# Weight low parts on VectorE in the front, later latent norms, earlier decays, a fifth bank and U tiles between the last queries

## The chip, the cores and the metric

One core of a Trainium2 chip runs the kernel. The metric is the device time of one execution in microseconds; a kernel's time is the median of several runs. Engines are named as in the profile: PE is TensorE's matrix engine, DVE is VectorE, ACT is ScalarE, POOL is GpSimd, SP issues most DMAs.

## The reference, cut to what matters

The input x has 512 rows (frames) of 1024 numbers, all float32. One layer is computed:

```python
h = rms_norm(x, g_mix);  proj = h @ w_in          # q_lat, kv_lat, k_rope, gq, gk, gv, g_lr, g_out, br
y_a = mla_attention(q_lat, kv_lat, k_rope, ...)    # norms of the latents, 8 heads, softmax
y_b = gla_mixer(gq, gk, gv, g_lr, g_out, ...)      # log_a = log_sigmoid(g_lr @ w_a2 + b_a2) / 16
x = x + (sigmoid(br_a) * (y_a @ w_branch_a) + sigmoid(br_b) * (y_b @ w_branch_b)) @ w_out
h = rms_norm(x, g_ffn)
s, idx = top_k(product_key_scores(h @ w_peer_q), 16)   # 8 heads x 2 halves, 128 keys each
y = sum over the best 16 experts of each head of gate * gelu(h . u[e]) * v[e]
out = rms_norm(x + y, g_final)
```

For 384 of the 512 rows the expert sum is computed densely over all 16384 experts (128 tiles of 128); the other 128 rows gather their experts' rows.

## The kernel before

**Products in three parts.** Every weight tile of 128x1024 float32 is loaded by SP into `raw` (3 buffers), split into a high part `whi` (ACT, `split_hi`, L236) and a low part `wlo` (`split_lo`, L242: raw minus high, on the engine in `lo_home[0]`, which is POOL until the dense U stage and DVE from there on). `mm3` multiplies with three matmuls for each of the 8 blocks: high with high, high weight with low activation, low weight with high activation. So the first two matmuls of a product `proj` need only `whi`; the third needs `wlo`. For the key tiles the order of operands is the other way and the second matmul needs the low part.

**Order.** The program is scheduled by hand: each engine runs its instructions in the order in which the code emits them. The weight tiles stand in one list (`want`): w1 tiles 0 to 5, the 8 key and value tiles `wkv`, w1 tiles 6 to 11, the query and key/value up-projections, gates, `wab`, `wo`, 16 `wpq` tiles, 128 `u` tiles. `weights(key)`, called at the start of a product, emits the low part of any tile whose high part is made already (`half`), then `run(1)`, one step of a list `later`; `further(key)`, called after the product, emits the high part of the tile after the next. So the low part of w1 tile k+1 is emitted at the start of product k, behind everything that the code emitted before it for the same engine.

**The front, in the order of the code.** Products 0 to 4 of w1 are the latents `ql`, each 24 matmuls into a bank of the PSUM group `pmm` (4 banks; `pk` and `pst` have 2 each). After product 2 the norm of x is made (`rstd`: a product with ones on PE, a DVE instruction, Ln and Exp on ACT with a table load before each, three DVE instructions), and three DVE multiplications evict products 0 to 2. After product 3 come its eviction and `rope_tables` (16 DVE instructions). Product 4 is evicted, then product 5 (`pm`) gives the gate's low-rank input and the rotary key: one small product, a copy `rcol`, six DVE instructions, then sums of squares of the latents (ACT squares, three DVE additions). Then the loop over 8 key tiles `c` (24 matmuls each; 4 banks `pv` of `pmm` and both of `pk` collect over all 8 tiles; POOL copies 32 rows of the rotary key in each). After tile 0 two `rstd` are started for the latents; their second halves and five latent norms (`latent_norm`: DVE, ACT, DVE) are put on `later`, one per following tile. After the loop `run()` empties `later`, ACT copies the four `pv` banks to `gv` (L511), four decay products with `wa2` follow (DVE `la`, ACT `z`), then Exp and Ln of `z`, a DVE instruction on `la`, and w1 products 6 and 7, the first of which takes the first bank of `pv`.

**The query stage.** For each of 16 `wpq` tiles: the product; for tiles 3 to 10 `normed(mt - 3)` (DVE multiplication, ACT high part, DVE low part of 128x384); ACT copies the product to `qq[mt]` (L909); `product_keys(mt - 1)`: PE multiplies by the keys, DVE makes top-16 values and indices for four row tiles (20 instructions). After the loop `some(P15)` runs 8 pieces (one U tile), `product_keys(15)`, then `some(3 * NC_D - P15)` two more U tiles; then `fx.close()` ends the front's SBUF pool, and `up_out` can evict the U products by a Gelu on ACT into `gx` (L975), which lies in a pool opened after that. `fill` then places U pieces by a cost count among the DVE work of `route` (the routing of the row tiles). What is left of the 128 U tiles goes in `trail` and among the `down` products at the end.

Of the kernel before, what the change touches and what calls it, by code (L numbers as in the profile page):

```python
# [10 lines left out]
F32 = mybir.dt.float32  # L11
# [5 lines left out]
AF = mybir.ActivationFunctionType  # L17
OP = mybir.AluOpType
# [20 lines left out]
PSH = ()  # L39
P15 = 8  # L40
G1, GO = 0.125, 0.5
LEAD = 3000.0
# [151 lines left out]
def body(ctx, tc, a, out):  # L194
# [32 lines left out]
    half = []  # L227
    lo_home = [pool]

# [61 lines left out]
    for mt in range(8):  # L291
        want(("wo", mt), a["wo"][mt].rearrange("p c m -> p (c m)"), 1024, v8)
    for mt in range(16):
        want(("wpq", mt), a["wpq"][mt].rearrange("p c m -> p (c m)"), 1024, v8)
    for e in range(128):
        want(("u", e), a["u"][e].rearrange("p c m -> p (c m)"), 1024, v8)
# [150 lines left out]
    for i in range(5):  # L447
        first.append(proj(("w1", i)))
        if i == 2:
            run()  # L450
            rstd(ssx, D, rX)
        if i >= 2:
            while first:
                dve.tensor_tensor(ql[i + 1 - len(first)], first.pop(0), rX, op=OP.mult)
        if i == 3:
            rope_tables()
# [17 lines left out]


    pv = [pmm() for _ in range(NT)]
    pk = [pmm("pk") for _ in range(2)]
    gv = fr.tile([128, NT, 512], F32, name="t6")
    kT = fr.tile([128, MH, T], F32, name="big2")
    for c in range(NC_D):  # L480
# [3 lines left out]
        for tt in range(NT):  # L484
# [4 lines left out]
            for n, (x, y) in enumerate(((0, 0), (0, 1), (1, 0))):  # L489
                pe.matmul(o, hs[x], w[y][:, 512:], start=f and tt % 2 == 0 and n == 0, stop=l and n == 2,  # L490
                          skip_group_check=True)
        if c == 0:
            rq = fr.tile([128, T], F32, name="rB", bufs=2)
# [13 lines left out]
            for i in range(5):  # L507
                later.append(lambda i=i: latent_norm(i))
    run()
    for tt in range(NT):  # L510
# [3 lines left out]
    further(("wkv", NC_D - 1))  # L514
    la = sb.tile([128, NT, 256], F32, name="la")
    z = sb.tile([128, NT, 256], F32, name="kd")
    for tt in range(NT):
        p = pmm("pst")
        pe.matmul(p[:, :256], lrT[0:GRANK + 1, tt * 128:(tt + 1) * 128], wa2, start=True, stop=True)
        dve.tensor_scalar(la[:, tt], p[:, :256], 0.0, 1.0 / TAU, op0=OP.min, op1=OP.mult)  # L520
        act.activation(z[:, tt], p[:, :256], AF.Abs)
    act.activation(z, z, AF.Exp, scale=-1.0)
# [315 lines left out]
    def normed(c):  # L838
        q = tmp()
        dve.scalar_tensor_tensor(q[:, GT:], x2[:, c, GT:], cc(C_GFFN + c), r2[:, GT:], op0=OP.mult, op1=OP.mult)  # L840
        split(h2d[c][0], h2d[c][1], q[:, GT:], dve)

# [56 lines left out]
    aside = [columns_of] + [lambda i=i: rows_of(i) for i in range(2)] + [lambda i=i: plain_rows_of(i) for i in range(2)]  # L899
    for mt in range(16):  # L900
        p = proj(("wpq", mt), h2x)
        if 3 <= mt < 3 + NC_D:
            normed(mt - 3)
        if mt > 2 and aside:
            aside.pop(0)()
        if mt == 0:
            rstd(ss, D, r2, defer=True)
        qq[mt] = tmp()
        act.activation(qq[mt], p, AF.Copy)  # L909
        if mt:  # L910
            product_keys(mt - 1)
    run()
    assert not aside
    ups = iter(range(128))
# [29 lines left out]
    def some(n):  # L944
        for _ in range(n):
            if left[0]:
# [3 lines left out]
                if c == NC_D - 1:  # L950
                    left[0] -= 1

    some(P15)
    product_keys(15)
    some(3 * NC_D - P15)
    lo_home[0] = dve
    ax = ExitStack()
# [9 lines left out]
    def up_out(keep=0):  # L967

        while len(pend) > keep:
            e, p = pend.pop(0)  # L970
            if e < NB[0]:
                g = pa.tile([128, ND], F32, name="gx", bufs=GX)
            else:
                g = ga[e] = dn.tile([128, ND], F32, name="gf", bufs=NF)
            act.activation(g, p[:, GT:], AF.Gelu)  # L975
            if e < NB[0]:
                act.dma_start(gad[e], g)


# [457 lines left out]
```

## Time and profile before

| | us |
|---|---|
| median of 3 runs (1653.6 to 1656.72) | 1655.02 |
| the profiled execution, its time | 1650.91 |
| its span from first to last instruction | 1649.1 |
| PE busy | 1611.3 |
| DVE busy | 1251.9 |
| ACT busy | 727.9 |
| POOL busy | 340.1 |

PE and DVE instructions are issued through a helper that counts their cost, so that nearly all of them have its line, L161; they are told apart by their tiles. The mean granted clock of TensorE was 0.995 of full speed. A matmul's row has its start and a modelled length; matmuls overlap, so the distance from start to start tells what one costs. A row with [x <-ENGINE tile] says that the engine was idle for x us before it, and who ended that.

### The profile page before, as it was taken

The page shows a single profiled execution, that of the slowest core. Times are in us where ns is not written, and L with a number is a line of the kernel's source. Part 1 is how long each engine was busy: PE and PEld are TensorE (multiplying, and loading weights), DVE is VectorE, ACT ScalarE, POOL GpSimd, SP SyncE. Part 2 cuts the span into 40 slices and gives each one's busy share as a digit, 9 for nine tenths or more (in the row PEclk, how much of TensorE's full clock was granted, in tenths as well). Part 3 has the DMA queues.
Part 4 walks back from the last instruction along what each step waited for, and adds up shares of the span by engine and source line. Part 5 has one row for each costly group of instructions (what it writes and reads, how often), then busy time and mean ns, then how long its engine had stood idle before and what let it go on. Part 6 is the DMA issues. An engine that isn't in the chain of part 4 may idle for free.

```text
span 1649.1 us, 23157 instructions
## 1 busy us (share of the span) xinstructions
PE 1611.3 (98%) x8505; PEld 1400.6 (85%) x8505; DVE 1251.9 (76%) x2528; ACT 727.9 (44%) x1251; POOL 340.1 (21%) x237
## 2 busy tenths in 40 slices
PE   7999999999989999999999999999999999999998
PEld 5777656888878899999999998888888888888876
DVE  6724575353789989988988747788888788888695
ACT  5442544334332645555555444344444444444343
POOL 4532143445324000000010001111111111112110
PEclk9999999999999999999999999999999999999999
DMA  5222112443332578878889998999999999999994
GB/s 178 64 77 77 52 58 90 168 146 98 132 103 90 188 277 282 285 277 309 278 302 336 331 369 312 332 370 342 396 340 384 347 380 351 397 329 360 346 343 150
DMA packets 156178, 414.11 MB, mean 251 GB/s; under 512 B 11975, under 2 KB 89928, under 8 KB 138016
## 3 DMA queue, kind: packets, MB, share of 16 engines
q1 hardware_dynamic: 121504, 234.02, 41.3%
q0 software_dynamic: 18576, 134.57, 21.7%
q10 hardware_dynamic: 15984, 44.05, 7.0%
q8 instruction: 66, 1.08, 0.3%
q14 instruction: 48, 0.39, 0.1%
HBM read 361.21 MB, written 51.38 MB: 250 GB/s over the span
## 4 chain that ended last, share of the span: by engine, by line
PE 83%; DVE 9%; DMA 2%; issue 2%; ACT 2%; POOL 0%; ACTq 0%; SPq 0%; DVEq 0%; POOLq 0%
PE pmm L161 59%; PE pst L161 13%; PE pk L161 11%; DVE kd L161 3%; DVE la L161 2%; DVE tmp L161 2%; DMA ga<-gad 1%; DMA gad<-gx 1%; DVE rB L161 0%; DVE r L161 0%; DVE act_lo L161 0%; ACT whi L236 0%; POOL wlo L242 0%; DVE rows L161 0%; DMA raw<-in_w 0%
## 5 line engine op out<-in xcount | busy, mean ns | idle before, releaser
L161 PE MATMUL pmm<-act_hi,whi 128*128 128x384 f32 (+1 forms) x992 | 355.5, 358 | 12.9 <-ACT act_hi L328 8.1
L161 PE MATMUL pmm<-act_hi,wlo 128*128 128x384 f32 (+1 forms) x992 | 347.6, 350 | 4.3 <-DVE wlo L161 4.3
L161 PE MATMUL pmm<-act_lo,whi 128*128 128x384 f32 (+1 forms) x992 | 347.3, 350 | 0.5 <-DVE act_lo L161 0.5
L996 POOL DMA_INDIRECT rows<-in_uv,gidx x128 | 132.9, 1038 | 935.9 <-DVE gout L161 884.7
L236 ACT ACTIVATE whi<-raw 128x1024 fp32r<-128x1024 f32 (+1 forms) x202 | 209.9, 1040 | 108.8 <-PE pmm L161 48.0
L242 POOL TENSOR_TENSOR wlo<-raw,whi 128x1024 fp32r<-128x1024 f32 (+1 forms) x77 | 182.4, 2371 | 292.5 <-ACT whi L236 255.8
L161 DVE TENSOR_TENSOR wlo<-raw,whi 128x1024 fp32r<-128x1024 f32 x125 | 152.7, 1222 | 87.3 <-ACT whi L236 85.7
L161 PEld LDWEIGHTS pmm<-act_hi,whi 128*128 128x128 f32 x992 | 188.4, 190 | 28.5 <-ACT act_hi L328 8.1
L161 PEld LDWEIGHTS pmm<-act_hi,wlo 128*128 128x128 f32 x992 | 188.1, 190 | 14.5 <-DVE wlo L161 4.9
L161 PE MATMUL pmm<-vlo,chi 128*128 128x512 f32 x512 | 199.9, 390 | 0.4 <-DVE vlo L161 0.2
L161 PE MATMUL pmm<-vhi,chi 128*128 128x512 f32 x512 | 199.4, 389 | 0.0
L161 PE MATMUL pmm<-vhi,clo 128*128 128x512 f32 x512 | 199.2, 389 | 0.0
L161 PEld LDWEIGHTS pmm<-act_lo,whi 128*128 128x128 f32 x992 | 188.4, 190 | 9.3 <-DVE act_lo L161 1.0
L161 DVE SCALAR_TENSOR_TENSOR gout<-rows,gact,gout 128x1024 f32<-128x1024 f32 x128 | 164.2, 1283 | 0.0
L161 DVE TENSOR_TENSOR vlo<-vraw,vhi 128x1024 fp32r<-128x1024 f32 x128 | 156.3, 1221 | 0.0
L161 DVE SCALAR_TENSOR_TENSOR rows<-rows,hrep 128x1024 f32<-128x1024 f32 x128 | 156.2, 1220 | 0.0
L1252 ACT ACTIVATE vhi<-vraw 128x1024 fp32r<-128x1024 f32 x128 | 134.0, 1049 | 26.3 <-DMA vraw<-in_v 25.8
L161 PE MATMUL pmm<-t,whi 128*128 128x512 f32 x448 | 141.8, 397 | 0.0
L161 PEld LDWEIGHTS pmm<-vlo,chi 128*128 128x128 f32 x512 | 96.1, 188 | 22.8 <-DVE vlo L161 2.9
L1008 ACT ACTIVATE gact<-gact 128x1 f32<-128x1 f32 x128 | 26.0, 203 | 197.8 <-DVE rows L161 197.7
L161 PEld LDWEIGHTS pmm<-vhi,clo 128*128 128x128 f32 x512 | 96.1, 188 | 18.7
L161 PEld LDWEIGHTS pmm<-vhi,chi 128*128 128x128 f32 x512 | 96.1, 188 | 18.6
(269 smaller groups left out, 2811.1 us busy)
## 6 DMA issues: line engine op xcount, KB each, us to landing
raw<-in_u SPq DMA_DIRECT2D x128, 512.0 KB
vraw<-in_v SPq DMA_DIRECT2D x128, 512.0 KB
gt<-gd SPq DMA_DIRECT2D x32, 768.0 KB
gd<-gs ACTq DMA_DIRECT2D x11, 2048.0 KB
gad<-gx ACTq DMA_DIRECT2D x96, 192.0 KB
ga<-gad SPq DMA_DIRECT2D x96, 192.0 KB
raw<-in_w SPq DMA_DIRECT2D x28, 512.0 KB
raw<-in_wpq SPq DMA_DIRECT2D x16, 512.0 KB
```

The costliest lines, as they stand in the source:

```text
L161: return f(*args, **kw)
L236: act.activation(hi[:, :n], raw[:, :n], AF.Copy)
L242: (lo_eng or lo_home[0]).tensor_tensor(lo[:, :n], raw[:, :n], hi[:, :n], op=OP.subtract)
L996: pool.indirect_dma_start(out=rows[n], out_offset=None, in_=a["uv"], in_offset=bass.IndirectOffsetOnAxis(ap=gidx[:, n:n + 1], axis=0))
L1008: act.activation(g, g, AF.Gelu)
L1252: act.activation(hi, vraw[n], AF.Copy)
```

## The change

1. `lo_home` starts with DVE, not POOL: all low parts up to the last `wo` tile are made by DVE. For the query stage it is set to POOL, as it was, and to DVE after it.
2. The fifth product of w1 goes to a bank of `pk`, not to the fifth place of `pmm`.
3. The two `rstd` of the latents and their five norms are queued after key tile 2, not after tile 0.
4. The four decay products, with their DVE and ACT instruction each, stand after key tiles 3 to 6 and no longer behind the loop and the `gv` copies; `la` and `z` are allocated earlier.
5. `normed` makes its low part on POOL, not on DVE.
6. The first two U tiles stand in the list of weights before `wpq` tiles 13 and 15, and their products run there. After `product_keys(15)` two further U tiles run, each with its low parts on POOL and with `up_out(LAG)` behind it, which evicts what is more than three products old. Five U tiles instead of three are then done when the cost count starts.

```diff
+AMID = (13, 15)
-    lo_home = [pool]
+    lo_home = [dve]
     for mt in range(16):
+        for e, at in enumerate(AMID):
+            if at == mt:
+                want(("u", e), ...)
         want(("wpq", mt), ...)
-    for e in range(128):
+    for e in range(len(AMID), 128):
         want(("u", e), ...)
-        first.append(proj(("w1", i)))
+        first.append(proj(("w1", i), bank="pk" if i == 4 else "pmm"))
+    la = sb.tile([128, NT, 256], F32, name="la")
+    z = sb.tile([128, NT, 256], F32, name="kd")
-        if c == 0:
+        if c == 2:
             ...   # rstd(sq_q), rstd(sq_kv), five latent_norm on later
+        if c >= 3 and c - 3 < NT:
+            tt = c - 3
+            p = pmm("pst")
+            pe.matmul(p[:, :256], lrT[0:GRANK + 1, tt * 128:(tt + 1) * 128], wa2, start=True, stop=True)
+            dve.tensor_scalar(la[:, tt], p[:, :256], 0.0, 1.0 / TAU, op0=OP.min, op1=OP.mult)
+            act.activation(z[:, tt], p[:, :256], AF.Abs)
     run()
     ...       # gv copies, further(("wkv", 7))
-    ...       # the same four decay products
-        split(h2d[c][0], h2d[c][1], q[:, GT:], dve)
+        split(h2d[c][0], h2d[c][1], q[:, GT:], pool)
+    lo_home[0] = pool
     for mt in range(16):
+        some(NC_D * AMID.count(mt))
         p = proj(("wpq", mt), h2x)
         ...
     some(P15)
     product_keys(15)
-    some(3 * NC_D - P15)
-    lo_home[0] = dve
     ...       # srt scaled, fx.close(), up_out defined
+    for _ in range(2):
+        some(NC_D)
+        while half:
+            split_lo()
+        up_out(LAG)
+    lo_home[0] = dve
```

## Rows read from the trace of the kernel before

**Rows 1.** The page: busy time, share and instructions of each engine.
```profile
PE 1611.3 (98%) x8505; PEld 1400.6 (85%) x8505; DVE 1251.9 (76%) x2528; ACT 727.9 (44%) x1251; POOL 340.1 (21%) x237
```
**Rows 2.** PE's waits: for whom, us in total, times, longest us.
```profile
PE pk L161 <- ACT tmp L909: 4.1, 4, 1.3
PE pmm L161 <- ACT x L678: 3.4, 8, 1.1
```
**Rows 3.** Timeline of PE, products 3 and 4: start us, us, instruction, [idle before].
```profile
34.08 0.39 PE L161 MATMUL pmm<-act_lo,whi 128*128 128x512 f32 x1
34.31 0.39 PE L161 MATMUL pmm<-act_hi,wlo 128*128 128x512 f32 x1
37.65 0.47 PE L161 MATMUL pmm<-act_hi,whi 128*128 128x512 f32 x1 [2.95 <-DVE t L161]
...
39.41 0.63 PE L161 MATMUL pmm<-act_hi,whi 128*128 128x512 f32 x1
39.84 0.63 PE L161 MATMUL pmm<-act_lo,whi 128*128 128x512 f32 x1
```
**Rows 4.** Timeline of DVE around products 3 to 5.
```profile
34.04 2.73 DVE L161 SCALAR_TENSOR_TENSOR r<-tmp,r 128x512 f32<-128x512 f32 x1
36.81 2.48 DVE L161 TENSOR_TENSOR t<-pmm,r 128x512 f32<-128x512 f32 x4
...
48.58 0.69 DVE L161 TENSOR_TENSOR t<-pmm,r 128x512 f32<-128x512 f32 x1
...
51.45 0.16 DVE L161 COPY rcol<-pst 128x4 f32<-128x4 f32 x1 [2.18 <-PE pst L161]
...
55.73 3.92 DVE L161 TENSOR_TENSOR tmp<-tmp 128x512 f32<-128x512 f32 x3
```
**Rows 5.** The page's groups of low parts: xcount | busy us, mean ns | idle before.
```profile
L242 POOL TENSOR_TENSOR wlo<-raw,whi 128x1024 fp32r<-128x1024 f32 (+1 forms) x77 | 182.4, 2371 | 292.5 <-ACT whi L236 255.8
L161 DVE TENSOR_TENSOR wlo<-raw,whi 128x1024 fp32r<-128x1024 f32 x125 | 152.7, 1222 | 87.3 <-ACT whi L236 85.7
```
**Rows 6.** Timelines of PE, ACT and DVE, key tiles to w1 product 6.
```profile
59.79 2.05 PE L161 MATMUL pst<-tmp,ones 128*128 128x512 f32 x2 [1.18 <-DVE tmp L161]
...
66.97 0.63 ACT L341 ACTIVATE rB<-rB 128x512 f32<-128x512 f32 x1
...
73.63 0.74 DVE L161 SCALAR_TENSOR_TENSOR tmp<-t,cst,rB 128x512 f32<-128x512 f32 x1
...
76.56 1.09 DVE L161 SCALAR_TENSOR_TENSOR tmp<-t,cst,rB 128x512 f32<-128x512 f32 x1
...
88.18 0.69 ACT L511 ACTIVATE t<-pmm,rcol 128x512 f32<-128x512 f32 x1 [3.27 <-PE pmm L161]
...
91.57 1.12 PE L161 MATMUL pst<-wa,lrT 17*128 17x256 f32 x4
...
93.29 1.13 PE L161 MATMUL pst<-wa,lrT 17*128 17x256 f32 x4 [0.59 <-ACT kd L521]
...
98.79 1.23 DVE L161 SCALAR_TENSOR_TENSOR la<-kd,la 128x1024 f32<-128x1024 f32 x1 [3.92 <-ACT kd L523]
```
**Rows 7.** Timeline of DVE in the attention.
```profile
207.60 2.87 DVE L161 SCALAR_TENSOR_TENSOR rB<-tmp,rB 128x512 f32<-128x512 f32 x1 [1.38 <-POOL tmp L605]
```
**Rows 8.** Timeline of DVE in the query stage.
```profile
476.24 0.60 DVE L161 SCALAR_TENSOR_TENSOR tmp<-x,cst,r 128x384 f32<-128x384 f32 x1
...
484.25 0.60 DVE L161 SCALAR_TENSOR_TENSOR tmp<-x,cst,r 128x384 f32<-128x384 f32 x1
485.44 0.56 DVE L161 TENSOR_TENSOR act_lo<-tmp,act_hi 128x384 fp32r<-128x384 f32 x1 [0.59 <-ACT act_hi L323]
```
**Rows 9.** Timelines of PE and ACT, last keys and first U tiles.
```profile
525.12 1.13 PE L161 MATMUL pk<-t,tmp 128*128 128x128 f32 x8 [0.19 <-DVE tmp L161]
...
538.43 1.28 ACT L975 ACT_TABLE_LOAD   x1 [7.03 <-DVE kd L161]
...
543.18 0.44 PE L161 MATMUL pmm<-act_hi,wlo 128*128 128x384 f32 x1 [2.29 <-DVE wlo L161]
```

More of the change, by code (lines that the diff above doesn't have):

```diff
@@ L293, in body @@
     for mt in range(16):
+        for e, at in enumerate(AMID):
+            if at == mt:
+                want(("u", e), a["u"][e].rearrange("p c m -> p (c m)"), 1024, v8)
         want(("wpq", mt), a["wpq"][mt].rearrange("p c m -> p (c m)"), 1024, v8)
-    for e in range(128):
+    for e in range(len(AMID), 128):
         want(("u", e), a["u"][e].rearrange("p c m -> p (c m)"), 1024, v8)
@@ L514, in body @@
     further(("wkv", NC_D - 1))
[L515 to L521, printed above, removed]
     act.activation(z, z, AF.Exp, scale=-1.0)
@@ L899, in body @@
     aside = [columns_of] + [lambda i=i: rows_of(i) for i in range(2)] + [lambda i=i: plain_rows_of(i) for i in range(2)]
[L900 to L913, printed above, removed]
     ups = iter(range(128))
@@ L951, in some @@
                     left[0] -= 1
+    lo_home[0] = pool
+    for mt in range(16):
+        some(NC_D * AMID.count(mt))
+        p = proj(("wpq", mt), h2x)
+        if 3 <= mt < 3 + NC_D:
+            normed(mt - 3)
+        if mt > 2 and aside:
+            aside.pop(0)()
+        if mt == 0:
+            rstd(ss, D, r2, defer=True)
+        qq[mt] = tmp()
+        act.activation(qq[mt], p, AF.Copy)
+        if mt:
+            product_keys(mt - 1)
+    run()
+    assert not aside
     some(P15)
     product_keys(15)
-    some(3 * NC_D - P15)
-    lo_home[0] = dve
     ax = ExitStack()
```

## The prediction

> **What bounds the kernel now.** The page comes first: PE is busy in 98% of the span [rows 1]. What PE does is the same after the change, matmul for matmul, so the time can only move by what PE waits and by stretches in which its clock is at the lower of its two levels. Its waits come second [rows 2], and the timeline tells where they are: in the front (rows 3, 4 and 6 below), in the attention behind ACT's exponentials, in the query stage behind ACT's copy at L909, and at the first U tiles. The dense stages from 550 to 1600 us have next to none, so nothing is to be had there. I therefore walk through the places at which PE waits, and ask of each what comes last there after the change. The sum is made against the profiled execution (1650.91 us) and then put on the median of the runs, 1655.02; the two differ by 4.1 us, and I take the difference that I find for both.
>
> Two prices are needed throughout. [...] A low part costs 1.22 us on DVE and 2.37 us on POOL [rows 5].
>
> **Low parts on DVE, and the fifth bank.** POOL holds DVE up: the last instruction of the norm, which takes 0.69 us where POOL is idle, took 2.73 us beside a low part on POOL [rows 4], and in the attention the same kind took 2.87 [rows 7]. So 2.04 us are won there. But an engine takes its instructions in the order of the code, and the low parts now stand in DVE's line. PE's wait before product 4 (2.95 us, until the first eviction has freed a bank, at 37.65) [rows 3] goes with the fifth bank. What is next there: the low part of product 4's own tile is emitted at the start of product 3, which is behind the norm and the three evictions. The norm ends at 34.04 + 0.69 = 34.73, three evictions (2.48 us for four [rows 4], 1.9 for three) end at 36.65, the low part at 37.9. PE can do two matmuls and waits for it from 35.0 on. Twenty-two are left: 5.0 us and 1.6 of slow clock, so product 4 ends at 44.5, where it ended at 37.65 + 24 x 0.23 + 1.6 = 44.7 before. The bank brings nothing.
>
> Product 5 is worse. Its low part is emitted at the start of product 4, behind the eviction of product 3 and all of `rope_tables`, which run from 36.81 + 2.48 = 39.3 until the next eviction at 48.58, 9.3 us [rows 4]. From 37.9, the eviction (0.7) and those 9.3 us last until 47.9, the low part until 49.05. Product 5 starts at 44.5 with two matmuls, idles for 4.1 us and ends at 49.05 + 5.0 + 1.6 = 55.7. Before, it ended at 50.3 (DVE got `rcol`, 1.2 us later, at 51.45 [rows 4]). That is **+5.4 us**. With its low part on POOL product 5 had no wait at all.
>
> **Key tiles, norms and decays.** Count from the end of product 5. `rcol` starts 1.2 us later, and it, the six instructions and the three additions take 51.45 to 57.8, 6.35 us, if the additions (3.92 us for three [rows 4], beside a low part on POOL) take 0.7 each. Only then comes the low part of key tile 1, 0.92 us as an estimate for its 768 of 1024 columns: at 8.5 us. Key tile 0 occupies PE from 1.1 to 5.3, so PE waits 3 us in key tile 1 and is slow after it. Here POOL still copies 32 rows for each tile. A DVE instruction took 1.09 instead of 0.74 us beside such work [rows 6]: between 0 and 4 x 0.35 = 1.4 us for the four on the path, of which I take 0.7.
>
> A key tile costs 4.25 us: seven between 61.84 and 91.57 [rows 6]. Tiles 1 and 2 end at 8.5 + 4.0 + 1.6 + 4.15 = 18.25 us. The two products with ones there (2.05 us before, behind a wait of 1.18 [rows 6]) find their sums ready and cost 0.9. The wait after tile 0 is gone, as intended; it is in the 44.1 us that this stretch took before, from 50.3 to the end of the decays at 94.4 [rows 6].
>
> What comes last is now on the other side of the loop. From the second product with ones to the last Exp it took from 59.79 to 67.60 [rows 6], and DVE adds 3 x 0.7. In the change the first `z` stands between the two norms on ACT and needs the decay product behind key tile 3, done 5.6 us after tile 2; then ACT has `z` (0.4), a high part (0.8), and Ln and Exp (0.63 each [rows 6]) with a table load of 1.28 each [rows 9], DVE its 2.1: the second norm is made 12.7 us after tile 2. Then DVE has, in order: three `la` (0.43 each, an estimate for 256 columns), the low parts of key tiles 6 and 7 and of w1 tile 6 (0.92, 0.92, 1.22), four latent norms of 0.74 + 0.70 + 0.69 and the fifth up to ACT's high part (1.4): 14.4 us. ACT copies the first `gv` (0.69 [rows 6]) only behind that fifth norm: 27.8 us after tile 2. PE has been done with its five tiles and four decays after 0.9 + 4 x 4.6 + 4.15 = 23.4. Product 6 takes the bank that this copy frees, so PE idles for 4.4 us. Before, all five norms were done within the loop. The stretch takes 18.25 + 27.8 = 46.05 us instead of 44.1: **+1.9**, with the copies **+2.6**; the slow clock behind the idle time is **+1.6**. Then the low part of w1 tile 7 stands behind the DVE instruction on `la`, which waits for Exp and Ln: it ended at 100.0 before [rows 6]. Product 6 now starts at 101.7 and ends at 108.8, and product 7 wants its low part at 109.2. Three copies (to 103.5), a high part, Exp, a table load, Ln, `la` and the low part itself (1.05 + 1.05 + 1.28 + 1.05 + 1.23 + 1.22 = 6.9) give 110.4: **+1.2**.
>
> Front: 5.4 + 2.6 + 1.6 + 1.2 = **+10.8**, between +7 (no slow stretch that matters, no copies) and +12.
>
> **Up-projections, attention.** Behind the rotary additions DVE has one low part more before the second bank of `pk` is freed: **+1.1**, from 0 to 1.2 [rows 5]. In the attention POOL's low parts no longer hold DVE. Eight waits for exponentials cost 3.4 us, the longest 1.1 each, behind `rB` of 2.87 us [rows 2, 7]. Two of these and their surroundings go: **-2.5**, between 0 (DVE's own 1.22 us in the same place) and -3.4. The `gate`, `wab` and `wo` stages have a whole product for each low part and DVE is half idle: 0.
>
> **Query stage.** Where `normed` stands, DVE takes 484.25 - 476.24 = 8.0 us for a tile, PE 24 x 0.23 and 1.13 for the keys [rows 9], 6.6. PE then waits for ACT's copy, which is behind the high part of `normed`: 4.1 us in four waits [rows 2, 8], 4.8 with some 0.2 each until the matmuls flow. With the low part on POOL, DVE is spared the 0.56 and the 0.59 us of waiting [rows 8], leaving 6.9: the four waits go, **-4.8**, at least -3.5. Before the last keys DVE held PE for another 0.19 us [rows 9]: **-0.2**.
>
> [...]
>
> **U tiles.** The cover moves. Before, the last keys start at 525.12 and three U tiles follow (12.5 us); then the next one waits for a bank, which the first Gelu frees once DVE has finished the keys at 538.4 and ACT has loaded a table, and for its low part until 543.18 [rows 9]: 4.1 us and 1.5 of slow clock. After, three U products already hold three of the four banks when the last keys start. One more follows, and the next waits for the same Gelu. DVE is not behind any more and ends the keys about 7.7 us after their start, the Gelu is done at 9.5; PE is out of work at 5.2. That is 4.3 us and 1.5 of slow clock. No low part is late there, since POOL makes it. **0**, from -4 to +2. Five tiles instead of three ahead of the routing change how many are left for `trail`, not PE's work: 0.
>
> **Sum.** 10.8 + 1.1 - 2.5 - 4.8 - 0.2 + 0 = +4.4 us: 1655.3 for the profiled execution, **1659.4** for the median. The gentle ends together (7 + 0 - 3.4 - 4.8 - 0.2 - 4) give 1649.6, the hard ones (12 + 1.2 + 0 - 3.5 + 2) 1666.7; such ends rarely fall together, so the case by itself holds from 1653 to 1665.
>
> **The rivals.** First, faster: DVE's line does not bind in the front, low parts are there when PE asks. It decides at 44.9 us: is the low part of product 5 ready when its first two matmuls are done? Then the idle time of 4.1 us there and the 3 + 1.6 in key tile 1 are gone: 1659.4 - 8.7 = 1650.7. For it: POOL's hold on DVE is as large as told above, and DVE is idle before 51.45 for 2.18 us. Against it: the eviction of product 4 stood behind `rope_tables` in the same way, its product done at 44.7 and itself begun at 48.58 [rows 4]. Chance 0.2.
>
> Second, no change: the front is late, but restarts run at the full clock in the two places, key tile 1 and product 6, where a slow stretch of 1.6 us delays the end: 1656.2. For it: the slow stretch does not begin with the restart at 37.65 [rows 3], and a gap that is cut up may bring none. Against: the gap of 2.95 us brought one. Chance 0.25.
>
> Third, slower still: the multiplication of `normed` falls into a low part on POOL and is held for 2 us in each of eight tiles. DVE then needs 6.9 + 2.0 = 8.9 us a tile, 0.9 more than before, so the 4.8 us stay and up to 8 x 0.9 come on top, of which I take 5: 1669. It decides from the point at which DVE is over 1 us behind PE. Chance 0.1. [...]
>
> **How the numbers follow.** The forecast has 0.45. About 0.2% (3.3 us) is what a measurement can tell from no change. Faster: most of the first rival, 0.18. Same: the second rival and a part of the forecast's lower range, 0.30. Slower: the rest, 0.52. The range that should hold 8 in 10 goes from 1649 to 1666; it leaves out the third rival and the lower part of the first.
>
> **What would show it.** In the profile after, the third matmul of product 5 starts near 49 us behind a DVE low part, and w1 product 6 near 101 instead of 94.4, behind ACT's L511. In the query stage PE's waits for L909 are gone. One wait of some 4 us for `gx` stands among the first U tiles and none for a low part. I am wrong if product 5 runs without a gap, if norms end within the key tiles, or if the dense stages, which I count at zero, have changed length.

## The result and the profile after

| | before | after |
|---|---|---|
| median, us | 1654.31 | 1681.02 |
| the profiled execution, us | 1650.91 | 1675.06 |
| its span, us | 1649.1 | 1673.3 |

The change makes the kernel slower: the ratio is 1.016, with a 95% interval from 1.0124 to 1.0196. That is 26.7 us where the prediction had 4.4, and outside its range. The profiled execution is the fastest of four after the change (1675.06 to 1684.48), so its trace holds 24.2 of the 26.7. In the page of the kernel after, first the busy times, then the group of low parts on DVE, now 180 of them in place of the 125 of [rows 5] (22 are left on POOL, those of the query stage and of the first U tiles):

```profile
PE 1619.9 (97%) x8505; PEld 1409.2 (84%) x8505; DVE 1271.0 (76%) x2575; ACT 727.0 (43%) x1251; POOL 220.0 (13%) x190
...
L162 DVE TENSOR_TENSOR wlo<-raw,whi 128x1024 fp32r<-128x1024 f32 (+1 forms) x180 | 217.5, 1209 | 111.4 <-ACT whi L237 111.4
```

Next PE's waits after the change, to be read against [rows 2] (for whom, us in total, times, longest). Lines have moved by one to five.

```profile
PE pmm L162 <- DVE wlo L162: 14.0, 4, 4.7
...
PE pmm L162 <- ACT t L523: 6.3, 1, 6.3
PE pmm L162 <- ACT gx L980: 5.5, 1, 5.5
PE pk L162 <- DVE wlo L162: 2.7, 1, 2.7
PE pk L162 <- ACT t L743: 1.9, 1, 1.9
PE pmm L162 <- DVE clo L162: 1.7, 1, 1.7
...
PE pmm L162 <- ACT x L683: 1.5, 8, 0.3
PE pmm L162 <- DVE vlo L162: 1.0, 2, 0.6
```

The four waits for L909 are gone, and those for `x` fell from 3.4 to 1.5. In their place stand 16.7 us in five waits for low parts on DVE and three single waits of 1.9 to 6.3 us. Before, there were two waits for low parts on DVE, in a line that [rows 2] does not show:

```profile
PE pmm L161 <- DVE wlo L161: 4.3, 2, 2.3
```

To see where the whole difference lies I take, from each matmul's start to the next one's, what exceeds the median distance of its kind; that counts waits and slow clock together. How the matmuls are sorted into kinds moves single rows by up to some 4 us, and the differences between the two columns by up to 1.6.

| stretch of the span | before, us | after, us |
|---|---|---|
| 40 to 160, front | 10.4 | 24.4 |
| 160 to 280, up-projections and attention | 9.7 | 15.7 |
| 440 to 520, query stage | 5.9 | 1.2 |
| 520 to 600, first U tiles | 6.6 | 8.6 |
| 960 to 1040, behind the routing | 2.4 | 6.6 |
| 1560 to 1640, end | 2.1 | 4.8 |
| all | 51.7 | 75.0 |

With the first matmul 1.0 us later (at 9.14; in kernels with an unchanged beginning it came between 8.05 and 9.30, so that is not the change) this makes the 24.2 us between the spans.

### The profile page after: what moved, and what is told of

Same layout as the page of the kernel before. It is cut to its first block, busy times and chain, and to the rows that moved or that the text cites. A ratio compares the mean times of both kernels' runs of the same rounds, so it can differ in the third digit from the quotient of the medians.

```text
span 1673.3 us, 23129 instructions
## 1 busy us (share of the span) xinstructions
PE 1619.9 (97%) x8505; PEld 1409.2 (84%) x8505; DVE 1271.0 (76%) x2575; ACT 727.0 (43%) x1251; POOL 220.0 (13%) x190
## 4 chain that ended last, share of the span: by engine, by line
PE 87%; DVE 6%; DMA 3%; ACT 2%; issue 1%; SPq 0%; ACTq 0%; DVEq 0%
PE pmm L162 64%; PE pst L162 13%; PE pk L162 10%; DVE tmp L162 1%; DMA gad<-gx 1%; DMA ga<-gad 1%; DMA vraw<-in_v 1%; DVE wlo L162 1%; DVE rows L162 1%; DVE t L162 0%; DVE la L162 0%; DVE kd L162 0%; DMA raw<-in_w 0%; DVE vlo L162 0%; DVE big L162 0%
## 5 line engine op out<-in xcount | busy, mean ns | idle before, releaser
L162 PE MATMUL pmm<-act_hi,whi 128*128 128x384 f32 (+1 forms) x1016 | 364.8, 359 | 21.3 <-ACT act_hi L332 9.1
L162 PE MATMUL pmm<-act_hi,wlo 128*128 128x384 f32 (+1 forms) x1016 | 357.1, 351 | 10.3 <-DVE wlo L162 10.3
L162 PE MATMUL pmm<-act_lo,whi 128*128 128x384 f32 (+1 forms) x1016 | 356.1, 351 | 0.5 <-DVE act_lo L162 0.5
L162 DVE TENSOR_TENSOR wlo<-raw,whi 128x1024 fp32r<-128x1024 f32 (+1 forms) x180 | 217.5, 1209 | 111.4 <-ACT whi L237 111.4
L162 PEld LDWEIGHTS pmm<-act_hi,whi 128*128 128x128 f32 x1016 | 194.0, 191 | 36.0 <-ACT act_hi L332 9.1
L162 PEld LDWEIGHTS pmm<-act_hi,wlo 128*128 128x128 f32 x1016 | 193.8, 191 | 20.8 <-DVE wlo L162 11.4
L162 PEld LDWEIGHTS pmm<-act_lo,whi 128*128 128x128 f32 x1016 | 193.9, 191 | 9.1 <-DVE act_lo L162 1.0
L162 PE MATMUL pst<-vlo,chi 128*128 128x512 f32 x256 | 99.8, 390 | 0.0
```

Of the source, the lines that this page charges most:

```text
L162: return f(*args, **kw)
```

## The experiments

Each ratio is to the kernel before, timed beside the run. The last column is the ratio less one, times 1655 us.

| run | what it is | ratio | 95% interval | loss (+) or gain (-), us |
|---|---|---|---|---|
| e1_front | front half of the change | 1.0137 | 1.0113 to 1.0162 | +22.7 |
| e2_query | the other half | 1.0013 | 1.0000 to 1.0027 | +2.2 |
| e3_lows | low parts on DVE alone | 1.0069 | 1.0047 to 1.0091 | +11.4 |
| e9_attention | the same, up to the key up-projection only | 1.0022 | 1.0011 to 1.0033 | +3.6 |
| e5_later | bank, later norms, earlier decays; low parts on POOL | 1.0007 | 0.9992 to 1.0021 | +1.2 |
| e6_decays | after, decays back behind the loop | 1.0113 | 1.0089 to 1.0138 | +18.7 |
| f1_z_first | after, `z` ahead of `la` | 1.0133 | 1.0113 to 1.0152 | +22.0 |
| f2_norms_c0 | after, norms back to key tile 0 | 1.0089 | 1.0065 to 1.0113 | +14.7 |
| e4_norms | normed low part on POOL alone | 0.9944 | 0.9925 to 0.9964 | -9.3 |
| e7_no_amid | e2_query without U tiles among the queries | 0.9978 | 0.9962 to 0.9994 | -3.6 |
| e10_lead | e2_query with LEAD 7200 | 0.9985 | 0.9974 to 0.9995 | -2.5 |
| e8_bank | e4_norms and the fifth bank | 0.9928 | 0.9906 to 0.9950 | -11.9 |
| e11_norms_c1 | e8_bank, norms after key tile 1 | 0.9934 | 0.9920 to 0.9947 | -10.9 |
| e12_weigh | e8_bank, weights behind the last U tiles | 0.9916 | 0.9901 to 0.9930 | -13.9 |

**The two halves.** e1_front is the kernel before with parts 1 to 4 of the change, and `lo_home` back on POOL ahead of the query loop; e2_query is the kernel before with parts 5 and 6.

> The front half of the change alone: all low parts up to the last wo tile on VectorE, the fifth bank, the latent norms after key tile 2, the decays between the key tiles; the query stage and the U tiles as in the kernel before. Theory (the trace of the changed kernel): the loss is in the front and the attention, +1 before the first product, +14.0 between 40 and 160 us and +6.0 between 160 and 280 us, so about +20 us against the kernel before. Rival (the sum of the prediction for these parts, 10.8 + 1.1 - 2.5): +9.4 us, and the rest of the 26 us comes from the parts at the other end.

> The other half alone: the norm's low part in the query stage on GpSimd, two U tiles between the last queries and two more behind them; the front as in the kernel before. Theory: -4.8 us in the query stage, +2.0 at the first U tiles, +4.3 at the tiles behind the routing (PE's wait of 4.7 us for a low part near 994 us) and +2.8 at the end (VectorE's waits for rows from DRAM near 1620 us), in all +4 us. Rival: the last two come from where the DMAs happen to fall when all is 20 us later, and not from the number of tiles that are left; then they are gone here and it is -2.8 us.

Measured: +22.7 and +2.2, together 24.9 of the 26.5 that the whole change costs by its ratio, a difference inside the intervals. The front half's theory holds, and its trace has the waits of the kernel after in the same places (24.2 us between 40 and 160, 15.6 between 160 and 280). e2_query's own two long waits, at the first U tile and behind the routing, are there too (5.5 and 4.1 us), and with them 2.1 us at the end; so these do not come from the front's being late.

**Low parts on DVE.** e3_lows changes one line, e9_attention gives the low parts back to POOL before the attention:

```
-    lo_home = [pool]
+    lo_home = [dve]
...
+    lo_home[0] = pool          # e3_lows: ahead of the loop over mt; e9_attention: ahead of weights("wk")
```

> One edit alone: the low parts up to the last wo tile on VectorE. Theory: VectorE's own line holds them, in the front (product 5 behind the rope tables, key tile 1 behind the additions) and in the attention: product 5's third matmul near 49 us with a wait of about 4 us, one in key tile 1, and the attention 4 to 6 us longer: +10 to +14 us. Rival (the prediction's rows for GpSimd holding VectorE): the attention gives back 2.5 us, so +5.4 + 1.1 - 2.5 = about +4 us.

> Low parts on VectorE as in e3_lows, but back on GpSimd from the key up-projection on, so that none of VectorE's low parts lies in the attention. Theory: the attention's loss (9.7 us of waits before, 15.9 in e3_lows) comes from low parts that stand in VectorE's line behind rotary additions and behind score reductions that themselves wait for PE; it goes, and what is left is product 5's wait in the front: e3_lows (+9 to +11 us) less 6, so +3 to +5 us. Rival (the prediction's): low parts on GpSimd hold VectorE in the attention, and taking them away is worth 2.5 us, so bringing them back costs that: +11 to +14 us.

Measured: +11.4 and +3.6. PE's waits from 160 to 215 us, in e3_lows:

```profile
PE pk L161 <- ACT t L738: 1.9, 1, 1.9
PE pmm L161 <- DVE wlo L161: 1.8, 1, 1.8
PE pk L161 <- DVE t L161: 1.0, 1, 1.0
PE pmm L161 <- ACT x L678: 0.6, 3, 0.3
```

and in e9_attention:

```profile
PE pmm L161 <- ACT x L679: 0.6, 3, 0.3
PE pk L161 <- DVE t L161: 0.5, 1, 0.5
```

So the attention's loss is that of the low parts there. PE's waits are less than half of it: from 160 to 280 us they sum to 6.9 us after, 4.7 before. Nearly all of the rest is TensorE's clock. In the kernel after, the granted clock was 0.91 from 180 to 200 us and 0.91 from 200 to 220, behind idle times of 1.0 and 1.8 us; e3_lows has both stretches too (0.91 from 160 to 180, 0.93 from 180 to 200), and before and in e9_attention it was 1.00 from 160 to 280. At 0.91, 20 us do the work of 18.2, so the two stretches cost some 3.6 us, an estimate from the granted clocks. In the second the four products with ones take 3.27 us,

```profile
207.12 3.27 PE L162 MATMUL pst<-t,ones 128*128 128x512 f32 x4
```

where they took 1.88 before (from 187.02). DVE's timeline of the kernel after shows how the second row's wait arises:

```profile
204.47 0.69 DVE L162 TENSOR_REDUCE stat<-pmm 128x1 f32<-128x512 f32 x1
205.19 0.15 DVE L162 TENSOR_SCALAR stat<-stat 128x1 f32<-128x1 f32 x1
205.26 1.22 DVE L162 TENSOR_TENSOR wlo<-raw,whi 128x1024 fp32r<-128x1024 f32 x1
```

The low part of a gate tile stands behind the reductions of four score tiles, and these can only begin when PE has made the scores. Its high part had been ready for 6.5 us (in e3_lows it begins at 188.52 and takes 1.05, the low part begins at 196.02). PE runs its two matmuls at 203.98 and 204.32 and waits for the third until 206.53. In the kernel before, POOL made this low part at 181.13, right behind its high part. The longer hold of DVE by POOL was real (2.87 us [rows 7] for an instruction that took 0.69 at 231.41 after), but it cost less there than a place in DVE's line (e9_attention +3.6, e3_lows +11.4).

**The other parts of the front, with low parts on POOL.**

> Fifth bank, latent norms after key tile 2 and decays between the key tiles, with the low parts on GpSimd as in the kernel before: what the front half of the change is without its first edit. The two traces with and without these parts put them at +12 us when the low parts are on VectorE (e1_front less e3_lows). Theory: most of that comes from VectorE's line, where a key tile's low part waits for ScalarE's high part, that for the z copy, and that for VectorE's la (four waits of 1.2 to 1.4 us); with low parts on GpSimd VectorE doesn't wait there, and the parts cost +2 us or less. Rival: the norms start two key tiles (8.4 us) later, their five steps of 3.3 us each (VectorE beside GpSimd) end behind the loop, and product 6 starts about 3.6 us later than before and with a slow clock: +5 us or more.

Measured: +1.2, from -1.3 to +3.5. The theory's bound holds, but its trace, of the slowest of twelve executions, has something of both: the waits before product 4 and for the ones are gone (for one of 2.2 us in key tile 0), and product 6 waits 4.9 us for ACT's gv copy, as the rival has it (until 96.31, where it started at 94.34 before). Against e1_front less e3_lows (11.3 us) it shows that the same three parts cost some 10 us more where the low parts are on DVE. It shows too what POOL's low parts do: in DVE's timeline of e5_later

```profile
89.42 2.53 DVE L161 TENSOR_TENSOR t<-tmp,t 128x512 fp32r<-128x512 f32 x1 [1.26 <-ACT t L323]
```

and in POOL's of the same kernel

```profile
89.01 2.40 POOL L242 TENSOR_TENSOR wlo<-raw,whi 128x1024 fp32r<-128x1024 f32 x1 [1.85 <-issue]
```

where the same instruction takes 0.69 in the kernel after (93.90, below).

**Decays, their order, and the norms.** Three kernels undo one thing each in the changed one: e6_decays puts the four decay products with `la` and `z` back behind the gv copies, f1_z_first swaps two lines, f2_norms_c0 changes one number.

```
 # f1_z_first
+            act.activation(z[:, tt], p[:, :256], AF.Abs)
             dve.tensor_scalar(la[:, tt], p[:, :256], 0.0, 1.0 / TAU, op0=OP.min, op1=OP.mult)
-            act.activation(z[:, tt], p[:, :256], AF.Abs)
 # f2_norms_c0
-        if c == 2:
+        if c == 0:
```

> The changed kernel with the decays back behind the loop and the gv copies; all else stays. Theory: the chain la, z, high part, low part between the key tiles is gone, so the latent norms run at 2.9 us each with their low part instead of 4.5, the first gv copy ends 5 us earlier, and then the decay products want 3 us of PE themselves: 2 to 4 us faster than the changed kernel, about +23 us against the kernel before. Rival: VectorE's own instructions set the pace (norms and low parts, 14.4 us), the chain hides beside them, and the decays behind the loop add their 3 us: +27 to +30.

> The changed kernel with two lines swapped: between the key tiles ScalarE's z is emitted before VectorE's la, so that la waits for z and not z for la. Nothing else changes, each engine has the same instructions. Theory: the price of the decays between the key tiles is the order (la, which stands behind a latent norm, then z, then the high part behind z, then the low part behind that, for which VectorE waits 1.2 to 1.4 us four times): with z first the high part is early, VectorE doesn't wait for it, the first gv copy ends some 5 us earlier and product 6 starts at 102 to 104 us instead of 108.1: 4 to 6 us faster than the changed kernel, so +20 to +23 against the kernel before. Rival: it is the instructions themselves (four la of 0.4 us, z in ScalarE's line before the norms' Ln and Exp) and the late start of the norms: within 1.5 us of the changed kernel, +25 to +28.

> The changed kernel with the latent norms queued after key tile 0 again; the decays stay between the key tiles and all else as changed. Theory: the sum of the runs (decays moved back gives 7 us, the low parts alone cost 11, the query half 2, of 27) leaves some 5 us for the later norms and the fifth bank when the low parts are on VectorE; with the norms two tiles earlier they end near the last key tile, product 6 waits 2 us at most, and PE waits for the sums of squares after key tile 0 as before (2 to 3 us): 4 to 6 us faster than the changed kernel, +20 to +23. Rival: the chain of la, z, high part and low part takes 4.5 us for each latent step wherever the norms begin, so product 6 waits as long: within 1.5 us of the changed kernel, +25 to +28.

Here is the chain between the key tiles in the kernel after, on DVE

```profile
89.98 0.42 DVE L162 TENSOR_SCALAR la<-pst 128x256 f32<-128x256 f32 x1
91.58 0.96 DVE L162 TENSOR_TENSOR wlo<-raw,whi 128x768 fp32r<-128x768 f32 x1 [1.18 <-ACT whi L237]
92.45 0.75 DVE L162 SCALAR_TENSOR_TENSOR tmp<-t,cst,rB 128x512 f32<-128x512 f32 x1
93.90 0.69 DVE L162 TENSOR_TENSOR t<-tmp,t 128x512 fp32r<-128x512 f32 x1 [0.70 <-ACT t L327]
94.51 0.42 DVE L162 TENSOR_SCALAR la<-pst 128x256 f32<-128x256 f32 x1
```

and on ACT:

```profile
90.43 0.38 ACT L520 ACTIVATE kd<-pst 128x256 f32<-128x256 f32 x1 [2.55 <-DVE la L162]
90.71 0.84 ACT L237 ACTIVATE whi<-raw 128x768 fp32r<-128x768 f32 x1
```

`z` (written into `kd`) starts 0.03 us after `la` ends, though both only read the bank. The high part stands behind `z`, the low part waits for it, and so one latent step takes 4.53 us (89.98 to 94.51). `la` and `z` of a step never overlap here, and in f1_z_first `la` starts 0.03 us after `z` instead (94.62 after 94.20 and 0.39); why one read has to wait for the other is not shown. In e6_decays, where `la` is gone from DVE's line, a step takes 3.05 us:

```profile
87.13 0.95 DVE L162 TENSOR_TENSOR wlo<-raw,whi 128x768 fp32r<-128x768 f32 x1
88.00 0.75 DVE L162 SCALAR_TENSOR_TENSOR tmp<-t,cst,rB 128x512 f32<-128x512 f32 x1
89.44 0.69 DVE L162 TENSOR_TENSOR t<-tmp,t 128x512 fp32r<-128x512 f32 x1 [0.70 <-ACT t L327]
90.18 0.96 DVE L162 TENSOR_TENSOR wlo<-raw,whi 128x768 fp32r<-128x768 f32 x1
```

From the products with ones to the first gv copy it takes 24.0 us there (76.04 to 100.01), against 31.7 after (75.68 to 107.40) and 29.7 in f1_z_first (77.44 to 107.14). So of the 7.7 us that the decays add to this chain, the order of `la` and `z` makes 2.0, less than the 5 I expected. The rest is `la` itself and where it stands: with `z` first DVE waits 0 to 0.5 us for the high part, but `la` waits for `z`, and `z` for PE's next decay product (1.25 us before the last `la`), and the latent step stands behind it. The timed difference of f1_z_first to the kernel after is inside the intervals, and product 6 starts within 0.3 us of it. e6_decays was timed 7.8 us below the kernel after (18.7 against 26.5), more than its theory, but the two intervals overlap (1.0089 to 1.0138, 1.0124 to 1.0196). In its trace product 6 starts 2.4 us earlier (105.69): the decays' second half waits 3.7 us for banks that `z` frees behind the copies. So 2.4 us are shown, and more is not.

f2_norms_c0 gives the most, 12 us. Its PE timeline:

```profile
99.20 0.50 PE L162 MATMUL pmm<-act_hi,whi 128*128 128x512 f32 x1 [0.66 <-ACT t L523]
...
107.60 0.50 PE L162 MATMUL pmm<-act_hi,wlo 128*128 128x512 f32 x1 [2.21 <-DVE wlo L162]
```

Product 6 waits 0.66 us instead of 6.3, and the time between `la`, `z` and low parts is hidden beside the key tiles: a latent step takes 5.0 us there (`la` at 84.19 and 89.19), each `la` waiting 0.38 us for PE's decay product. The late norms are thus the costliest part of the change after the low parts, once DVE has these to make. Undoing either takes away the same wait, so the two gains don't add: together they would be 19.8 us, where these parts and the fifth bank cost 11.3 (e1_front less e3_lows). The profiled execution of f2_norms_c0 is 5.2 us below that of the kernel after, not 12: it is 1.1 us above its own median, the other 6.0 below. So the order of the parts is shown, and the size of this one is not.

**The query half.** e4_norms and e7_no_amid:

```
-        split(h2d[c][0], h2d[c][1], q[:, GT:], dve)
+        split(h2d[c][0], h2d[c][1], q[:, GT:], pool)     # e4_norms: this alone
-AMID = (13, 15)
+AMID = ()                                                # e7_no_amid, in e2_query
```

> One edit alone: the norm's low part in the query stage on GpSimd. Theory: the four waits of PE for ScalarE's copy of the queries go, -4.8 us (and -0.2 before the last keys). Rival: the multiplication of the norm is held by GpSimd's low parts; then VectorE needs up to 2 us more per tile and the time stays within 1 us of the kernel before or is above it.

> The query half alone (as e2_query), but with no U tile between the last queries; the norm's low part on GpSimd and the two U tiles with low parts on GpSimd behind the last keys stay. The normed low part alone gave -10 us and with the U tiles +1.7. Theory: the two U tiles among the queries hold three of the four banks when the last keys start, PE then waits 5.5 us for the first Gelu, and two tiles more are done ahead of the routing; without them it is near the normed low part alone, -8 to -10 us. Rival: the loss comes from the two tiles behind the last keys, their low parts on GpSimd, which come before the next pieces and leave the same number too many ahead of the cost count: it stays at 0 to +2 us.

Measured: -9.3 and -3.6. PE's waits from 440 to 545 us are, in e4_norms:

```profile
PE pmm L161 <- DVE wlo L161: 0.8, 1, 0.8
```

in e7_no_amid:

```profile
PE pmm L162 <- POOL wlo L243: 1.8, 1, 1.8
```

in e2_query:

```profile
PE pmm L162 <- ACT gx L979: 5.5, 1, 5.5
```

In the kernel before they were 8.1 us: the 4.1 for L909, 2.3 for a low part and 0.2 [rows 2, 9], and 1.5 for the first Gelu. One edit takes away nearly all of them, the U tile's too: DVE is no longer behind PE when the last keys come, so the Gelu can start while PE still has its three U tiles. The two U tiles between the queries use up this cover. In the kernel after, PE's timeline

```profile
548.98 1.05 PE L162 MATMUL pk<-t,tmp 128*128 128x128 f32 x8
...
559.74 0.69 PE L162 MATMUL pmm<-act_hi,whi 128*128 128x384 f32 x1 [5.54 <-ACT gx L980]
```

and ACT's

```profile
557.90 1.28 ACT L980 ACT_TABLE_LOAD   x1 [7.79 <-DVE kd L162]
559.19 0.49 ACT L980 ACTIVATE gx<-pmm 128x384 f32<-128x384 f32 x1
```

show it: the Gelu waits for DVE's last keys, and behind the last keys PE has one U tile, done at 554.20. Taking the two tiles out gives 5.8 us, the theory's place; but not the whole way to e4_norms. The other 5.7 us come with the two tiles behind the last keys, whose low parts POOL makes. The traces don't settle how: e7_no_amid waits 1.0 us more here and 3.5 us more behind the routing (6.9 against 3.4), but the profiled executions of the two take the same time (1649.85 and 1649.54), and e4_norms' is the longest of its runs.

**Behind the routing, and the end.**

> The query half (as e2_query) with the constant LEAD at 7200 instead of 3000, so that one U tile less runs under the routing and one more behind it; 96 instead of 100 U results then go through DRAM, as in the kernel before. Theory: the waits at the end (1600 to 1627 us, 4.3 us of them) come with the 100, since the last group of four then has its loads in the stretch in which the DMA engines are fullest; with 96 they fall to the 1.5 to 2 us of the other kernels with 96: 2.5 to 3 us faster than e2_query, about -1 us against the kernel before. Rival: the end is as it is by chance of the DMAs, and the trail is one tile longer: no change within 1 us, +1 to +2.

> As e8_bank, and the first four multiplications of U results by their weights (VectorE, on rows that come back from DRAM) stand behind the last U tiles and not between them. Theory: the wait of PE for a low part near 965 us (2.0 us in the kernel before, 4.7 in the changed one, 3.6 in e8_bank) is VectorE's line again: the low part stands behind a multiplication that waits 10 us for its rows. It goes, and PE waits at most 1 us for the next tile's high part: -2.5 to -4 us against e8_bank, so -14 to -16. Rival: the next weight tile itself, whose load is queued behind the same rows, is what comes last: PE waits as long one tile later, 0 against e8_bank.

e10_lead gives 4.7 us against e2_query. The page's row of the results that go to DRAM is, in e2_query,

```profile
gad<-gx ACTq DMA_DIRECT2D x100, 192.0 KB
```

and in e10_lead

```profile
gad<-gx ACTq DMA_DIRECT2D x96, 192.0 KB, 5.1
```

PE's waits from 1560 us on are 2.1 us in two waits in e2_query (for `clo` and `vlo`, as in the kernel after) and none in e10_lead. That the 100 are the cause fits these two, but the number alone does not decide: with 96, PE waits 1.3 us there in e9_attention and 1.0 in e12_weigh, and with 100 it waits 0.9 in f2_norms_c0. The constant moves other things too, so the cause of the waits at the end is not shown.

The wait behind the routing is another matter: 2.0 us before, 4.7 after, 4.1 in e2_query, 6.9 in e7_no_amid, which has 96 as before. It does not go with the number. DVE's timeline in the kernel after:

```profile
995.03 1.66 DVE L162 TENSOR_TENSOR ga<-ga,gt 128x384 f32<-128x384 f32 x3 [7.91 <-DMA ga<-gad]
997.00 0.56 DVE L162 TENSOR_TENSOR ga<-ga,gt 128x384 f32<-128x384 f32 x1 [0.32 <-DMA ga<-gad]
997.48 1.22 DVE L162 TENSOR_TENSOR wlo<-raw,whi 128x1024 fp32r<-128x1024 f32 x1
```

The low part stands behind four multiplications that wait for rows from DRAM. e12_weigh moves these behind the last U tiles:

```
-    for n in range(4):
-        weigh(n)
     g_load(1)
     trail(0)
+    for n in range(4):
+        weigh(n)
```

Its PE waits there are, instead of 3.6 us in e8_bank:

```profile
PE pk L161 <- DVE wlo L161: 0.6, 1, 0.6
PE pk L161 <- ACT whi L236: 0.6, 1, 0.6
```

So that is one more case of DVE's order. In time it is 2.0 us better than e8_bank, less than expected and within the intervals; between 1520 and 1640 us PE loses 2.2 us more than in e8_bank, counted as in the table above.

**A version that beats both.** e8_bank and e11_norms_c1 keep from the change what paid.

> The kernel before with the norm's low part in the query stage on GpSimd and the fifth bank; low parts in the front on GpSimd. Theory: PE's wait of 2.95 us before product 4 goes, product 5 ends earlier, and VectorE, which waits 2.18 us for its small product, gives all of that on: about -2 us against the normed low part alone (-10), so -12. Rival: the rope tables and the eviction of product 4 are what VectorE is busy with, PE waits as much at the next sum; 0 against it, so -10.

> As e8_bank (fifth bank, normed low part on GpSimd, low parts of the front on GpSimd), and the latent norms queued after key tile 1, not 0; decays behind the loop. Theory: the products with ones find their sums ready, so PE's two waits there (1.3 and 0.2 us) and the slow matmuls behind them go, some 3 us; the five latent steps end 4 us later, at about 88.5 us, PE is through the key tiles at 86 and the decays at 89, and the first gv copy at 89.2 holds product 6 by 1 us at most: -2 us against e8_bank, so -14. Rival: with the norms one tile later product 6 waits as in e5_later, where it cost 4.9 us with its slow clock at two tiles: +1 to +3 against e8_bank, so -9 to -11.

e8_bank: in its trace product 4 has no wait, and the first products with ones come 2.0 us earlier than in the profiled kernel before (55.50 against 57.49); the theory's 2 us are there, its timed 2.6 against e4_norms is inside the intervals. e11_norms_c1 took PE's waits for the ones away and got as much back behind the loop: the decays' second half waits 2.2 us (until 89.81). The rival's size holds, but the wait is the decays', not product 6's. The best time is that of e12_weigh at 0.9916, whose interval overlaps with that of e8_bank: the kernel before with the normed low part on POOL, the fifth bank, and the first four weightings later.

## Why the prediction was wrong, by its steps

The sign was right, and so was the reason that weighed most, that the low parts stand in DVE's line. Four terms failed, by 7.4, 3.2, 2.0 and 6.9 us; the largest is the attention.

The sums add 1.6 us (1.5 at the U tiles) of slow clock to each long idle time, and no run shows that as a fixed price. Behind the 2.95 us of [rows 3] the matmuls are 0.43 us apart from 38.99 to 41.97 (granted clock 0.50 from 39 to 41.9 us, 1.00 from 34 to 37.65), which does make 1.6. In the kernel after, those behind the waits of 2.69, 3.73 and 3.75 us in the front lost 1.5 to 1.6, those behind the 5.54 us for the Gelu some 2.4, and those behind the 6.29 us at product 6 some 3.

**Attention: -2.5 and +1.1 were predicted, +6.0 came.** The +1.1 was right (1.0 us for DVE's `t` in `pk`, at 180.60). The step that failed is "POOL's low parts no longer hold DVE", which priced what DVE gains and gave DVE's own 1.22 us as the bound of what it loses. What stands ahead of the low parts there, four score reductions that wait for PE, was not looked at. `rB` did become shorter (0.69 at 231.41 in place of the 2.87 of [rows 7]) and the waits for `x` fell by 1.9 us, as predicted; e9_attention shows that the place costs more than that. And the slow clock behind the new waits, some 3.6 us, stood in no term of this stretch.

**Key tiles and norms: product 6 was put at 101.7 and came at 108.13.** The products with ones came at 75.68, where I had 55.7 + 18.25 = 73.95; and from there the first gv copy ended after 32.4 us, not 27.8. I summed DVE's own durations to 14.4 us and let `z` and the high parts run beside them. In the trace DVE waits four times for a high part (1.18, 1.18, 1.18 and 1.40), and each latent step goes from DVE to ACT and back twice. The 1.2 us for the low part of w1 tile 7 did not come, since product 6 was late anyway; where product 6 starts earlier (f2_norms_c0) it is there, with 2.2 us. Product 6 starts 13.8 us later than before, 12.8 without the later first matmul. The slow clock behind its wait was priced at 1.6 us and cost some 3: the matmuls stay 0.43 us apart until 114.27 (granted clock 0.50 from 108 to 114.2 us). The kernel before loses 1.6 there too, which the prediction did not see (0.43 us apart from 110.47 to 113.45, granted clock 0.50). Together this is about the 14.0 of the table, where 10.8 was predicted.

**U tiles: 0 was predicted, +2.0 came.** PE ran out of work 5.2 us after the last keys, as predicted; the Gelu was done after 10.7, not 9.5, since DVE was still 2 us behind. That is inside the bounds given. What was missed is larger and lies in the comparison: `normed` on POOL would by itself have ended this wait (e4_norms), and I credited it with 5.0 us where it gave 9.3.

**Behind the routing and at the end: 0 was predicted, +4.2 and +2.7 came.** "Five tiles instead of three ahead of the routing change how many are left for `trail`, not PE's work" was true of PE's work and no reason about its waits, and "The dense stages from 550 to 1600 us have next to none" passed over one that was there. Of the 4.3 us for low parts on DVE before, this stood between 940 and 1005 us:

```profile
PE pmm L161 <- DVE wlo L161: 2.0, 1, 2.0
```

I did not follow it up. It became 4.7 us, and the clock, 1.00 behind it before, was 0.83 from 995 to 1005 us, another 1.7.

Right were these: product 5's third matmul at 49.05 (49.71 in the trace below) and +5.4 us for it (5.1 more between 40 and 160 us in e3_lows than before); the fifth bank, which brings nothing with DVE's low parts (the wait of 2.95 us became one of 2.69 two matmuls later); key tile 1's wait (3 predicted, 3.75) with its slow clock; the query stage, 4.7 us less (4.8 and 0.2 predicted), at 6.9 us a tile (DVE's multiplication of `normed` begins at 464.07 and next at 470.94). PE's timeline of the kernel after:

```profile
38.61 0.50 PE L162 MATMUL pk<-act_hi,wlo 128*128 128x512 f32 x1 [2.69 <-DVE wlo L162]
...
49.71 0.80 PE L162 MATMUL pmm<-act_hi,wlo 128*128 128x512 f32 x1 [3.73 <-DVE wlo L162]
...
65.86 0.50 PE L162 MATMUL pmm<-wlo,act_hi 128*128 128x512 f32 x1 [3.75 <-DVE wlo L162]
...
108.13 0.80 PE L162 MATMUL pmm<-act_hi,whi 128*128 128x512 f32 x1 [6.29 <-ACT t L523]
```

Of the rivals the first fell at the point it named: the low part of product 5 is not ready at 44.9. The second fell too: the slow clock followed both restarts. In key tile 1 it begins some 0.7 us after the restart (last section), and from the restart to the products with ones it takes 9.8 us, as priced with a slow stretch (4.0 + 1.6 + 4.15). The third did not occur: the multiplication of `normed` takes 0.60 us after as before (seven of them between 457 and 499 us), and POOL has been idle for some 2 us when each starts, so the condition was not met.

## What to carry to other kernels

Before work is moved to an engine with time to spare, list what stands ahead of it in that engine's line and what each of those instructions waits for; the instruction's own duration can be far below its price (in the kernel after PE waited 1.8 to 4.7 us for low parts of 0.96 to 1.22). Where a step goes back and forth between two engines, add the waits of both lines for each round, not the busy time of one. A new wait of TensorE can also bring a stretch of slow clock that costs as much as the wait (in the attention of the kernel after some 3.6 us behind waits of 1.0 and 1.8). And price each edit of a bundle alone: the best version here is a third of this change, and the rest cost more than that third won.

## What the runs showed of the hardware

Behind idle time of the same length the slow stretch was shorter in one run and longer in another. In the kernel after, the wait of 3.75 us before 65.86 is followed by

```profile
66.19 0.39 PE L162 MATMUL pmm<-whi,act_lo 128*128 128x512 f32 x1
...
66.95 0.63 PE L162 MATMUL pmm<-whi,act_hi 128*128 128x512 f32 x1
67.37 0.63 PE L162 MATMUL pmm<-wlo,act_hi 128*128 128x512 f32 x1
```

The first of these takes 0.23 us to the next start (66.42), as from 70 to 74 us, where the granted clock was 1.00; from 66.95 to 69.72 those of 512 columns are 0.43 us apart, and the granted clock was 0.57 from 66 to 70 us. In f1_z_first the same wait of 3.75 us is followed by

```profile
66.58 0.79 PE L162 MATMUL pmm<-wlo,act_hi 128*128 128x512 f32 x1 [3.75 <-DVE wlo L162]
67.17 0.63 PE L162 MATMUL pmm<-whi,act_lo 128*128 128x512 f32 x1
```

and the matmuls of 512 columns stay 0.43 us apart (68.23, 68.66, 69.09) until 72.07; the granted clock was 0.50 from 66 to 70 us and 0.71 from 70 to 74. What differs ahead of the two I did not find. From that restart to the products with ones it takes 10.9 us in f1_z_first and 9.8 in the kernel after, which is the same code up to there.

Short waits preceded it as well. In the attention of the kernel after it followed waits of 1.0 and 1.8 us (granted clock 0.91 in 20 us); in the kernel before, waits of 1.1 us there, before 212.25 and 239.66, brought none (granted clock 1.00).

GpSimd's copies of the rotary key lengthened VectorE's instructions less than its low parts did. Beside eight copies in a row (61.93 to 69.95 us in the kernel after) three additions took 2.72 us, 0.91 each, where one takes 0.69 alone and one such instruction took 2.53 beside a low part (e5_later, above).
